# A hybrid SSD/S5 layer step in fp32 halves: z stored without SiLU, norm sums set between blocks of the first output product, S5 loads written one batch earlier

## The chip, the core and the metric

The kernel runs on one core of a Trainium2 chip. TensorE (PE) does the matrix products and takes its weights through a load step of its own (PEld); VectorE (DVE), ScalarE (ACT) and GpSimd (POOL) do the element-wise work; SyncE (SP) issues nearly all DMA transfers, in one queue, in the order of the program. The metric is the device time of one launch in microseconds. The time before is the median of three runs, 1028.26 us (1025.12 to 1031.12).

## What is computed

One step of one decoder layer for T = 1056 tokens: 1024 of a prompt, and 32 of 8 samples with 4 tokens each. Cut to what matters here:

```python
n = rmsnorm(h, g_in)
z_a, xbc, dt_raw, z_b, u_b = split(n @ w_in)
# A: Mamba-2 SSD, 16 heads in 2 groups of 512 channels
x, B, C = split(silu(causal_conv(xbc)))
y = ssd_scan(x, dt, A, B, C) + D * x
y = y * silu(z_a)
ya = y * rsqrt(mean(y * y, of its group) + eps) * ssd_norm_g
# B: S5, 64 groups of 16 channels, a complex diagonal state of 64 each
g = gelu(s5_scan(u_b))
yb = g * sigmoid(g @ glu_w + glu_b) * silu(z_b)
h = h + concat(ya, yb) @ w_out
h = h + (p @ w_ple_proj) * sigmoid(rmsnorm(h, g_ple) @ w_ple_gate)
return rmsnorm(h, g_final), states
```

`z_a` and `z_b` are needed only late, as the factors `silu(z)`; each is 1024 channels by 1056 tokens.

## The kernel before

Channels lie on the 128 partitions, tokens along the row. A dense product runs in fp32 split into a high and a low half, so each block is 24 matmuls: 8 slices of the contraction times three (high by high, high by low, low by high). Weights come by DMA in 128x512 pieces (`wr`), ACT rounds them to the high half (`wh`) and DVE subtracts to get the low half (`wl`). Activations go through the same split: `opn` is the pair of halves of an operand of the output product, its high half copied on ACT and its low half subtracted on DVE.

The order of the instructions on each engine is fixed when the kernel is built: a scheduler places them by modelled times under the dependencies of the program and some pins (`issue_after`, and `behind`, which sets an instruction behind a given one on its engine). On the chip each engine then runs its own list in order, and a waiting instruction holds all that stand behind it. Times below are microseconds from the start of the profiled span.

- To about 213: norm of the input, the u tiles, the S5 coefficients.
- 213 to 475: the convolution tiles and 16 batches of S5 (`s5_batch`), four channel groups each. A batch loads `u8`, `mm` (512 KB of matrices, from `md` in DRAM), `om` and `h8` from a pool of two buffers each, so the loads of batch n can begin when the last products of batch n-2 (`yp`) have read theirs. It starts on PE with the products `vi` and `vr` from `mm`.
- 475 to 656: the SSD recurrence in 16 units, and among it the rest of the z tiles. All 16 z tiles are products of 352 columns or fewer, evacuated by `z_evac`: ACT takes tanh(z/2) from PSUM, DVE forms (tanh + 1) * z, which is 2 silu(z), and the tile `zt` goes to DRAM (`zb_d` for j below 8, `za_d` above).
- 656 to 742 (and its m = 0 from 622 on, among the SSD units): the GLU, m = 0 to 7. The evacuation loads the z_b tile back (`gzl`) and `g` (`gg`), and DVE multiplies up to `yb`. After each m, `za_apply(m)` loads the z_a tile (`zl`, three pieces of 352 columns, called c0 to c2), multiplies it into `x` of that m on DVE, squares the product on ACT and adds the square to `ysq` on POOL. The tiles `zt`, `gzl`, `gg` and `zl` share one ring of six buffers.
- `ya_norm(g)` is the norm of SSD group g: sums of `ysq` over partitions as 12 matmuls of one column (`nsp`), a root by twelve short DVE operations (`nv`, `ny`, `nt`), a broadcast by 12 matmuls (`nrb`), and 12 DVE multiplications into `x`. `ya_norm(0)` follows m = 3, `ya_norm(1)` the loop.
- 742 to 913: the output product as seven products of half size (a Strassen form), each of 8 blocks of 24 matmuls with 264 columns, written in `PROD`. The first, `b11`, multiplies x of group 0 and yb 0 to 3; later ones need x of group 1. A block goes to one of eight PSUM banks, three of them the ones of `psb`, which `nrb` uses too.
- 913 to the end: the gate, the last product and the final norm.

Of the kernel before, what the change touches and what calls it, by code (L numbers as in the profile page):

```python
# [24 lines left out]
CW = 352  # L25
# [15 lines left out]
def hymba_ssd_s5_kernel(  # L41
# [216 lines left out]
    def rstd_tok(chunks, n, eps=EPS, after=None, pause=None):  # L258

        sp = psa("nsp")  # L260
        tw = chunks[0][0].shape[1]
        gr = -(-tw // 128)
        gr += tw % gr > 0
        qt, w = tw // gr, gr * len(chunks)
        for c, sqs in enumerate(chunks):

            for i, q in enumerate(sqs):
                if pause and i == len(sqs) - 1:
                    pe_end[0] = after
                    pause()  # L270
                    after = pe_end[0]
                for j in range(gr):
                    with behind(after):
                        end = PE.matmul(out=sp[0:qt, gr * c + j:gr * c + j + 1], lhsT=q[:, qt * j:qt * j + qt],  # L274
                                        rhs=ones[:, 0:1], start=(i == 0 and j == 0),
                                        stop=(i == len(sqs) - 1 and j == gr - 1))
                    if after is not None:
                        after = pe_end[0] = end
        v, y, t = (nw_p.tile([128, 16], F32, tag=q, name=q, bufs=b)[0:qt, 0:w]
                   for q, b in (("nv", 2), ("ny", 3), ("nt", 2)))  # L280
        ts(v, sp[0:qt, 0:w], 1.0 / n, eps, ALU.mult, ALU.add)
# [453 lines left out]
    def z_evac(j):  # L735
        dst = zb_d[j] if j < 8 else za_d[j - 8]

        def evac(c, t0, n, ps):
            t = ev("zt", n)
            if j >= 8:  # L740
                act(t, ps, AF.Tanh, scale=0.5)
                v_mid[0] = stt(t, t, 1.0, ps, ALU.add, ALU.mult)
                dma(out=dst[:, t0:t0 + n], in_=t)
                return

            nn = min(n, NPT - t0)
# [16 lines left out]
    def za_apply(j):  # L763
        for c in range(3):
            t0 = CW * c
            t = ev("zl")
            dma(out=t, in_=za_d[j, :, t0:t0 + CW])
            y = xs[j][:, t0:t0 + CW]
            mul(y, t, y)
            if j % 4 == 0:  # L770
                if c == 0:
                    ysq["t"] = cvt("ysq")
                ysq[c] = ysq["t"][:, t0:t0 + CW]
                act(ysq[c], y, AF.Square)
            else:
                act(t, y, AF.Square)
                add(ysq[c], ysq[c], t, G)
# [3 lines left out]
    NJ = NB // 2  # L781

    def s5_batch(b):
# [4 lines left out]
        u8 = s5.tile([128, NB, 144], F32, tag="u8", name="u8")  # L788
        dma(out=u8, in_=ud[:, :, g0:g0 + NB].rearrange("s h g c -> (s h) g c"))
        mm = s5.tile([128, NB, 2, 128], F32, tag="mm", name="mm")  # L790
        dma(out=mm, in_=md[:, g0:g0 + NB])
        tm, wv = mm[:, :, 0], mm[:, :, 1]
        om = s5.tile([128, NJ, 2, 128], F32, tag="om", name="om")
        dma(out=om, in_=od[:, j0:j0 + NJ])
        h8 = s5.tile([128, 2, NJ, 9], F32, tag="h8", name="h8")
        dma(out=h8, in_=s5h9[:, :, j0:j0 + NJ])
# [195 lines left out]

    def ya_norm(g):

        rt = rstd_tok([[ysq[c]] for c in range(3)], 512, 4 * EPS)
        for c in range(3):
            rs = rstd_bcast(rt[:, 4 * c:4 * c + 4])
            for i in range(4):
                y = xs[4 * g + i][:, CW * c:CW * c + CW]
                stt(y, y, vc[:, V_NG + 4 * g + i:V_NG + 4 * g + i + 1], rs, ALU.mult, ALU.mult)  # L1000
# [65 lines left out]
    for i, nm in enumerate(MID):  # L1066
# [84 lines left out]
    for m in range(8):  # L1151
# [3 lines left out]
        def evac(c, t0, n, ps):  # L1155
            z = ev("gzl", n)
            dma(out=z, in_=zb_d[m, :, t0:t0 + n])
            t = ev("zt", n)
# [9 lines left out]
            for yv, a, b, s, s0 in ((y[:, 0:NPT], 0, nn, 8, t0 // 128),) + (((y[:, NPT:T], nn, n, 4, 0),) if nn < n else ()):  # L1168
                zv, tv = (r[:, a:b].rearrange("p (s c) -> p s c", c=128 if s == 8 else 8) for r in (z, t))
                stt(yv.rearrange("p (c s) -> p s c", s=s)[:, s0:s0 + zv.shape[1]], zv, 0.25, tv, ALU.mult, ALU.mult)  # L1170
# [14 lines left out]
    def banks():  # L1185
        return [f("psd")[:, 0:CQ] for f in (lambda n: psd_(), lambda n: psd_(), lambda n: psd_(), psa, psa, psb, psb, psb)]
# [23 lines left out]
    for j, (wb, blk) in enumerate(PROD):  # L1210
        bk = banks()
        nxt = []
        for i in range(4):
            hi, lo = take_w((wb, i))
            w_split = list(last_split)
            for c in range(2):
                ps = bk[2 * i + c]
# [31 lines left out]
        opn = nxt  # L1249
# [190 lines left out]
```

## Time and profile before

| | us |
|---|---|
| median of three runs | 1028.26 |
| lowest, highest | 1025.12, 1031.12 |
| the profiled execution | 1028.4 |
| its span, first to last instruction | 1026.6 |
| PE busy | 996.4 (97%) |
| DVE busy | 809.5 (79%) |
| ACT busy | 454.6 (44%) |
| POOL busy | 164.9 (16%) |
| granted clock of TensorE, mean | 0.994 |

The profiled execution agrees with the median to 0.1 us, so a sum made against it needs no scaling. PE's share says how little of the span is left to win: 30 us in which PE stood still. Busy time of the other engines matters only where PE waits for them. The granted clock is the share of full speed at which the chip let TensorE run; a stretch at 0.5 is one at the lower of its two levels.

### The profile page before, as it was taken

To read this page: it belongs to the slowest core of one execution; us is meant where nothing else is said; L and a number is where in the kernel's file an instruction comes from. 1 tells how busy PE (TensorE), PEld (TensorE's weight loads), DVE (VectorE), ACT (ScalarE), POOL (GpSimd) and SP (SyncE) were. 2 spreads that over 40 slices of the span, in tenths; PEclk is the share of its full clock that TensorE was granted. 3 is DMA by queue.
4 is the path that set the end of the run, shared out by engine and by line. 5 is a ranking of instruction groups with operands and counts; after the bars stand their busy time and mean duration, and the time that the engine had idled before them with its cause. 6 is when DMAs were issued, how large, how long until landed. Compare 5 with 4: busy or idle time off the path is not lost.

```text
span 1026.6 us, 19644 instructions
## 1 busy us (share of the span) xinstructions
PE 996.4 (97%) x7214; PEld 945.3 (92%) x7214; DVE 809.5 (79%) x1880; ACT 454.6 (44%) x1009; POOL 164.9 (16%) x183
## 2 busy tenths in 40 slices
PE   9999999999999989999999997999999999999997
PEld 8999999979899989899887886899999999999996
DVE  5889989675998978984687768868778879986466
ACT  5733223345453434354865436344345435464221
POOL 0000000000000000002144233121232015641221
PEclk9999999999999989999999999999999999999999
DMA  9633489774658687755366668675634323335123
GB/s 315 219 77 120 148 254 245 198 244 132 196 168 255 193 236 206 207 155 183 113 185 200 204 189 224 170 201 166 176 114 136 112 90 125 120 114 171 50 95 106
DMA packets 181072, 174.89 MB, mean 170 GB/s; under 512 B 47728, under 2 KB 145520, under 8 KB 180976
## 3 DMA queue, kind: packets, MB, share of 16 engines
q1 hardware_dynamic: 150944, 153.23, 50.1%
q10 hardware_dynamic: 30032, 20.40, 6.4%
q8 instruction: 57, 0.93, 0.4%
q14 instruction: 39, 0.32, 0.1%
HBM read 123.05 MB, written 54.73 MB: 173 GB/s over the span
## 4 chain that ended last, share of the span: by engine, by line
PE 54%; DVE 8%; DMA 6%; issue 4%; ACT 2%; SPq 1%; POOL 0%; POOLq 0%; DVEq 0%; ACTq 0%
PE psd L233 30%; PE psd L1221 15%; DMA mm<-md 2%; PE yp L312 2%; ACT ab L77 1%; DMA ab<-acs_d 1%; PE nrb L296 1%; PE yd L873 1%; DVE acc L92 1%; PE yo L922 1%; DMA gr<-gd 1%; PE st L925 1%; DVE x L92 1%; DVE sst L80 1%; PE nsp L274 1%
## 5 line engine op out<-in xcount | busy, mean ns | idle before, releaser
L233 PE MATMUL psd<-n_h,wl 128*128 128x352 f32 x840 | 274.3, 327 | 1.4 <-DVE wl L80 1.4
L233 PE MATMUL psd<-n_h,wh 128*128 128x352 f32 x840 | 274.8, 327 | 0.0
L233 PE MATMUL psd<-n_l,wh 128*128 128x352 f32 x840 | 274.5, 327 | 0.0
L1221 PE MATMUL psd<-opn,wh 128*128 128x264 f32 x896 | 164.6, 285 | 1.7 <-DVE opn L80 1.7
L233 PEld LDWEIGHTS psd<-n_h,wh 128*128 128x128 f32 x840 | 158.7, 189 | 6.4 <-issue 6.1
L233 PEld LDWEIGHTS psd<-n_h,wl 128*128 128x128 f32 x840 | 158.7, 189 | 5.6 <-issue 3.4
L233 PEld LDWEIGHTS psd<-n_l,wh 128*128 128x128 f32 x840 | 158.7, 189 | 3.2 <-issue 2.9
L1221 PEld LDWEIGHTS psd<-opn,wh 128*128 128x128 f32 x896 | 138.8, 188 | 2.1 <-DVE opn L80 2.1
L80 DVE TENSOR_TENSOR wl<-wr,wh 128x512 fp32r<-128x512 f32 x146 | 106.3, 755 | 39.4 <-ACT wh L77 34.1
L77 ACT ACTIVATE wh<-wr 128x512 fp32r<-128x512 f32 x147 | 85.4, 622 | 105.5 <-PE psd L233 64.9
L1221 PE MATMUL psd<-opn,wl 128*128 128x264 f32 x448 | 127.1, 284 | 0.0
L1221 PEld LDWEIGHTS psd<-opn,wl 128*128 128x128 f32 x448 | 84.3, 188 | 0.0
L77 ACT ACTIVATE ab<-ab,tok 128x128 f32<-128x128 f32 (+1 forms) x144 | 42.9, 379 | 51.7 <-DMA ab<-acs_d 37.0
L233 PE MATMUL psd<-g_h,wh 128*128 128x384 f32 (+1 forms) x168 | 54.4, 324 | 0.0
L233 PE MATMUL psd<-g_l,wh 128*128 128x384 f32 (+1 forms) x168 | 54.0, 321 | 0.0
L233 PE MATMUL psd<-g_h,wl 128*128 128x384 f32 (+1 forms) x168 | 53.9, 321 | 0.0
L233 PE MATMUL psd<-hg_h,gwh 128*128 128x400 f32 (+1 forms) x144 | 46.7, 324 | 0.0
L233 PE MATMUL psd<-hg_l,gwh 128*128 128x400 f32 (+1 forms) x144 | 46.4, 322 | 0.0
L233 PE MATMUL psd<-hg_h,gwl 128*128 128x400 f32 (+1 forms) x144 | 46.3, 322 | 0.0
L77 ACT ACT_TABLE_LOAD x27 | 34.6, 1283 | 25.0 <-DVE acc L92 12.6
L92 DVE SCALAR_TENSOR_TENSOR zt<-zt,psd 128x352 f32<-128x352 f32 (+2 forms) x56 | 25.9, 463 | 23.3 <-ACT zt L77 23.0
L80 POOL TENSOR_TENSOR xl<-xl,h 128x264 f32<-128x264 f32 x32 | 29.8, 936 | 84.1 <-DMA xl<-xT 34.9
(323 smaller groups left out, 2044.3 us busy)
## 6 DMA issues: line engine op xcount, KB each, us to landing
wr<-wall SPq DMA_DIRECT2D x128, 256.0 KB, 3.4
mm<-md SPq DMA_DIRECT2D x16, 512.0 KB, 5.9
wa<-wall SPq DMA_DIRECT2D x32, 256.0 KB, 4.5
ws_d<-wa SPq DMA_DIRECT2D x16, 512.0 KB, 5.1
ab<-acs_d SPq DMA_DIRECT2D x16, 512.0 KB, 5.0
wr<-ws_d SPq DMA_DIRECT2D x32, 256.0 KB, 2.8
ud<-ub ACTq DMA_DIRECT2D x8, 576.0 KB, 4.8
u<-ud SPq DMA_DIRECT2D x16, 288.0 KB, 5.0
```

The lines of the kernel that those rows point to most:

```text
L77: return S.activation(out=out, in_=in_, func=func, **kw)
L80: return (eng or V).tensor_tensor(out=out, in0=a, in1=b, op=op)
L92: return V.scalar_tensor_tensor(out=out, in0=a, scalar=s, in1=b, op0=op0, op1=op1)
L233: end = PE.matmul(out=ps, lhsT=a[:, ko + k, :], rhs=b, start=(i == 0), stop=(i == 3 * K - 1))
L274: end = PE.matmul(out=sp[0:qt, gr * c + j:gr * c + j + 1], lhsT=q[:, qt * j:qt * j + qt], rhs=ones[:, 0:1], start=(i == 0 and j == 0), sto ...
L296: end = PE.matmul(out=rb[:, qt * j:qt * j + qt], lhsT=y[:, j:j + 1].to_broadcast([qt, 128]), rhs=ident[0:qt, 0:qt], start=True, stop=True)
L312: self.last = f(*a, **kw)
L873: PE.matmul(out=yd[64 * (e % 2):64 * (e % 2) + 64, e // 2], lhsT=x1[:, e], rhs=mt[:, e], start=True, stop=True)
L922: PE.matmul(out=yo[:, i], lhsT=hg[:, 128 * i:128 * i + 128], rhs=ct[g][:, cols], start=True, stop=True)
L925: PE.matmul(out=st, lhsT=bk, rhs=x2.rearrange("p e q -> p (e q)"), start=True, stop=True)
L1221: PE.matmul(out=ps, lhsT=a[:, k, :], rhs=b, start=(k == 0 and q == 0), stop=(k == 7 and q == 2))
```

## The change

Three things are rewritten. First, `z_evac` stores z as it comes from the product (one ACT copy, no DVE step), and SiLU is taken on ACT after the tile has been loaded back: on `gzl` in the GLU, and on `zl` in `za_apply`. The factors that made up for 2 silu(z) go (0.25 to 0.5, and 4 eps to eps). The additions into `ysq` go from POOL to DVE. Second, `ya_norm(1)` is cut into pieces written among the blocks of the first output product and pinned there: the `nsp` sums of c0, c1 and c2 directly behind blocks 0, 1 and 2, the root after the third, all `nrb` broadcasts behind block 4. The operands and the order of the second product are turned so that its yb half comes first; `ya_norm(0)` moves from behind m = 3 to ahead of `za_apply(4)`. Third, the loads of an S5 batch are a function `s5_load`, called for the next batch at the end of the loop step before.

```diff
-    def rstd_tok(chunks, n, eps=EPS, after=None, pause=None):
+    def rstd_tok(chunks, n, after=None, pause=None):
...
+        return rstd_root(sp[0:qt, 0:w], n)
...
         def evac(c, t0, n, ps):
             t = ev("zt", n)
             if j >= 8:
-                act(t, ps, AF.Tanh, scale=0.5)
-                v_mid[0] = stt(t, t, 1.0, ps, ALU.add, ALU.mult)
+                act(t, ps)
                 dma(out=dst[:, t0:t0 + n], in_=t)
                 return
...
-                act(v, pv, AF.Tanh, scale=0.5)
-                v_mid[0] = stt(v, v, 1.0, pv, ALU.add, ALU.mult)
+                act(v, ps[:, a:b].rearrange("p (c s) -> p s c", s=ns))
...
             t = ev("zl")
             dma(out=t, in_=za_d[j, :, t0:t0 + CW])
+            act(t, t, AF.Silu)
             y = xs[j][:, t0:t0 + CW]
             mul(y, t, y)
...
-                add(ysq[c], ysq[c], t, G)
+                add(ysq[c], ysq[c], t)
...
+    def s5_load(b):
+        s5, g0, j0 = s5c_["p"], NB * b, NB * b // 2
...
+        s5c_[b] = u8, mm, om, h8
 
     def s5_batch(b):
...
+        if b not in s5c_:
+            s5_load(b)
+        u8, mm, om, h8 = s5c_.pop(b)
...
             s5_batch(nb)
             nb += 1
+        if i > 2 and nb < 16:
+            s5_load(nb)
...
             z = ev("gzl", n)
             dma(out=z, in_=zb_d[m, :, t0:t0 + n])
+            act(z, z, AF.Silu)
...
         yb.append(y)
+        if m == 4:
+            ya_norm(0)
         za_apply(m)
-        if m == 3:
-            ya_norm(0)
-        if m in (4, 5):
-            opn += operand("b11", range(4 * (m - 4), 4 * (m - 4) + 4))
-
-
-    ya_norm(1)
+        if m == 4:
+            opn = operand("b11", range(4, 8))
+        if m == 5:
+            opn = operand("b11", range(4)) + opn
...
+    def ya_piece(n):
+        if n < 3:
+            if n == 0:
+                ya1["sp"] = psa("nsp")
+            for j in range(4):
+                with behind(pe_end[0]):
+                    pe_end[0] = PE.matmul(out=ya1["sp"][0:88, 4 * n + j:4 * n + j + 1],
+                                          lhsT=ysq[n][:, 88 * j:88 * j + 88], rhs=ones[:, 0:1],
+                                          start=(j == 0), stop=(j == 3))
+        if n == 2:
+            ya1["rt"] = rstd_root(ya1["sp"][0:88, 0:12], 512)
+        if n == 4:
+            for c in range(3):
+                ya_scale(1, c, ya1["rt"])
...
-                        PE.matmul(out=ps, lhsT=a[:, k, :], rhs=b, start=(k == 0 and q == 0),
-                                  stop=(k == 7 and q == 2))
+                        with behind(pe_end[0] if j == 0 and 0 < 2 * i + c < 6 else None):
+                            end = PE.matmul(out=ps, lhsT=a[:, k, :], rhs=b, start=(k == 0 and q == 0),
+                                            stop=(k == 7 and q == 2))
+                        if j == 0 and 2 * i + c < 6:
+                            pe_end[0] = end
+                if j == 0 and 2 * i + c < 5:
+                    ya_piece(2 * i + c)
...
-                    nxt += operand(PROD[j + 1][1], range(2 * i, 2 * i + 2))
+                    nxt += operand(PROD[j + 1][1], [(2 * i + q + (4 if j == 0 else 0)) % 8 for q in range(2)])
...
-        opn = nxt
+        opn = nxt[4:] + nxt[:4] if j == 0 else nxt
```

What it moves, by the built order of the two kernels. PE, in the first output product, before (the third block, whose start waits for its weights, and then the norm sums of all three pieces, which wait for POOL):

```order
L1221 MATMUL psd<-opn,wh 128x264 [waits Activation_49]
L1221 MATMUL psd<-opn,wh 128x264
L1221 MATMUL psd<-opn,wl 128x264 [waits DVE_49]
...
L1221 MATMUL psd<-opn,wl 128x264 [waits DVE_49]
L274 MATMUL nsp<-cs,ysq 88x1 [waits Pool_49]
L274 MATMUL nsp<-cs,ysq 88x1 x3
```

PE at the end of the first block of that product, after:

```order
L1255 MATMUL psd<-opn,wh 128x264 x2
L1255 MATMUL psd<-opn,wl 128x264
L1213 MATMUL nsp<-cs,ysq 88x1 [waits DVE_49]
L1213 MATMUL nsp<-cs,ysq 88x1 x3
L1255 MATMUL psd<-opn,wh 128x264 [waits Activation_49]
L1255 MATMUL psd<-opn,wh 128x264
L1255 MATMUL psd<-opn,wl 128x264
```

The first sums have moved from the middle of the third block to the end of the first, ahead of the whole second block, and wait for DVE in place of POOL. ACT at the end of the GLU, before (`zt` is the GLU's last evacuation, `h4` the first product block's, `zl` from `x7` the three squares of `za_apply(7)`):

```order
L77 ACTIVATE wh_8774<-wr_8771 128x512 [waits DMAHW4_49]
L77 ACTIVATE zt_8675<-psd_8648,glb_5612 128x288 [waits DMAHW5_49,DMAHW2_49,DMAHW6_49,DVE_49,PE_49]
L77 ACTIVATE h4_8757<-psd_8762 128x264 [waits PE_49]
L77 ACTIVATE zl_8683<-x7_5345 128x352 [waits DMAHW3_49,DVE_49,Activation_49]
L77 ACTIVATE zl_8688<-x7_5345 128x352 [waits DMAHW4_49,DMAHW7_49,DVE_49,Pool_49]
L77 ACTIVATE zl_8693<-x7_5345 128x352 [waits DMAHW5_49,DVE_49]
```

and after:

```order
L77 ACTIVATE zt_8664<-psd_8636,glb_5580 128x288 [waits DMAHW5_49,PE_49]
L77 ACTIVATE zl_8672<-zl_8672 128x352 [waits DMAHW3_49,DVE_49]
L77 ACTIVATE h4_8694<-psd_8709 128x264 [waits PE_49]
L77 ACTIVATE opn_8770<-yb4_8091 128x528
L77 ACTIVATE opn_8773<-yb5_8289 128x528
L77 ACTIVATE zl_8678<-zl_8678 128x352 [waits DMAHW7_49,DMAHW4_49,DVE_49]
L77 ACTIVATE zl_8684<-zl_8684 128x352 [waits DMAHW5_49]
L77 ACTIVATE zl_8672<-x7_5325 128x352 [waits DVE_49]
```

The square of c0 now stands behind three Silus, the copy out of block 0 and two operand copies; on DVE the addition of c0 into `ysq` stands behind the two operand subtractions and the multiplications of c1 and c2 in the same way. SP in the convolution stage, around the loads of one S5 batch (n = 9), before:

```order
L181 DMA wa<-wall 128x2x256 [waits DMAHW6_49]
L162 DMA wr<-wall 128x512 [waits DMAHW7_49,DVE_49]
L794 DMA om<-od 128x512 [waits PE_49]
L789 DMA u_4378<-ud 128x576 [waits PE_49]
L791 DMA mm<-md 128x1024 [waits DMAHW2_49]
L852 DMA gd<-yt 128x544 [waits DMAHW3_49,Activation_49]
```

and after:

```order
L162 DMA wr<-wall 128x512 [waits DMAHW6_49,DVE_49]
L162 DMA wr<-wall 128x512 [waits DMAHW7_49,DVE_49]
L792 DMA om<-od 128x512 [waits DMAHW0_49,PE_49]
L788 DMA u_4241<-ud 128x576 [waits DMAHW1_49,PE_49]
L790 DMA mm<-md 128x1024 [waits DMAHW2_49]
L861 DMA gd<-yt 128x544 [waits DMAHW3_49,Activation_49]
```

The loads stand at the same place in the queue, between the weight loads and the store of `gd`, and still behind a wait for PE, which is the release of the buffers by batch n-2.

## Rows read from the trace of the kernel before

**Rows 1.** The page, busy time of each engine, share, instructions.

```profile
PE 996.4 (97%) x7214; PEld 945.3 (92%) x7214; DVE 809.5 (79%) x1880; ACT 454.6 (44%) x1009; POOL 164.9 (16%) x183
```

**Rows 2.** Busy time by stage: stretch, length, each engine's busy us (instructions), clock, DMA.

```profile
620.00:656.00 36.00, 29.24 (x195) 23.39 (x196) 33.63 (x60) 16.46 (x39) 13.05 (x9) 0.95 0.76 204
656.00:742.00 86.00, 86.00 (x557) 85.52 (x556) 64.67 (x130) 33.34 (x66) 16.07 (x16) 1.00 0.67 189
742.00:770.00 28.00, 28.00 (x242) 28.00 (x241) 21.88 (x47) 13.05 (x27) 7.95 (x9) 1.00 0.37 112
```

**Rows 3.** Waits of PE, whole span: waiter, releaser, us in total, times, longest.

```profile
PE vi L309 <- DMA mm<-md: 6.5, 4, 2.9
PE psd L247 <- ACT g_h L77: 3.9, 4, 2.4
...
PE psd L233 <- DVE wl L80: 1.4, 1, 1.4
PE vi L309 <- DVE tb L80: 1.2, 1, 1.2
```

**Rows 4.** The tile mm, its 16 loads.

```profile
DMA to landing us min/median/max: 4.8/5.9/6.8
```

**Rows 5.** Timeline, S5 batch 9: start, us, engine, line, operation [idle before].

```profile
354.83 0.38 PE L312 MATMUL yp<-u,mm 128*128 128x136 f32 x1
...
359.11 0.43 SPq L791 DMA_DIRECT2D mm<-md  x1
...
365.60 0.46 PE L309 MATMUL vi<-u,mm 128*64 128x136 f32 x1 [2.90 <-DMA mm<-md]
```

**Rows 6.** Timeline, end of the GLU and first output product.

```profile
742.18 0.40 PE L1221 MATMUL psd<-opn,wh 128*128 128x264 f32 x2
...
742.82 1.40 SPq L767 DMA_DIRECT2D zl<-za_d  x3
...
743.30 0.48 ACT L77 ACTIVATE zt<-psd,glb 128x288 f32<-128x288 f32 x1
...
745.29 0.39 ACT L77 ACTIVATE h<-psd 128x264 f32<-128x264 f32 x1 [1.51 <-PE psd L1221]
...
745.57 1.07 DVE L80 TENSOR_TENSOR x<-zl,x 128x352 f32<-128x352 f32 x2
...
747.40 0.74 DVE L80 TENSOR_TENSOR x<-zl,x 128x352 f32<-128x352 f32 x1 [0.77 <-DMA zl<-za_d]
...
749.87 1.97 PE L274 MATMUL nsp<-cs,ysq 128*88 128x1 f32 x24
...
758.34 5.99 DVE L92 SCALAR_TENSOR_TENSOR x<-x,vc,nrb 128x352 f32<-128x352 f32 x12 [0.43 <-PE nrb L296]
```

**Rows 7.** Groups by line and shape: count, busy us, mean ns, idle before.

```profile
L77 ACT ACTIVATE opn<-yb 128x528 fp32r<-128x528 f32 x28 | 17.2, 643 | 16.5 <-DVE yb L80 16.5
L80 DVE TENSOR_TENSOR opn<-yb,opn 128x528 fp32r<-128x528 f32 x28 | 20.8, 789 | 0.0
L80 DVE TENSOR_TENSOR x<-zl,x 128x352 f32<-128x352 f32 x24 | 12.6, 551 | 3.9 <-DMA zl<-za_d 3.5
L77 ACT ACTIVATE zl<-x 128x352 f32<-128x352 f32 x18 | 8.8, 496 | 22.2 <-DVE x L80 21.3 <-DMA wr<-wall 0.8
L77 ACT ACTIVATE zt<-psd 128x352 f32<-128x352 f32 x40 | 18.1, 451 | 19.5 <-PE psd L233 18.0 <-issue 1.4
L92 DVE SCALAR_TENSOR_TENSOR zt<-zt,psd 128x352 f32<-128x352 f32 (+2 forms) x56 | 25.9, 463 | 23.3 <-ACT zt L77 23.0
L77 ACT ACT_TABLE_LOAD x27 | 34.6, 1283 | 25.0 <-DVE acc L92 12.6
```

**Rows 8.** Busy time of two stretches behind a wait, columns as in rows 2.

```profile
365.00:371.00 6.00, 5.40 (x27) 5.07 (x28) 2.00 (x6) 1.22 (x4) 0.00 (x0) 0.50 1.03 228
371.00:374.00 3.00, 3.00 (x18) 3.00 (x18) 3.00 (x12) 0.78 (x4) 0.00 (x0) 0.87 0.36 96
638.00:642.00 4.00, 4.00 (x22) 3.72 (x19) 3.97 (x11) 3.53 (x12) 1.19 (x1) 0.57 0.70 182
```

More of the change, by code (lines that the diff above doesn't have):

```diff
@@ L278, in rstd_tok, with rstd_root @@
                         after = pe_end[0] = end
+        return rstd_root(sp[0:qt, 0:w], n)
+    def rstd_root(sp, n):
+        qt, w = sp.shape
         v, y, t = (nw_p.tile([128, 16], F32, tag=q, name=q, bufs=b)[0:qt, 0:w]
                    for q, b in (("nv", 2), ("ny", 3), ("nt", 2)))
-        ts(v, sp[0:qt, 0:w], 1.0 / n, eps, ALU.mult, ALU.add)
+        ts(v, sp, 1.0 / n, EPS, ALU.mult, ALU.add)
         ts(y.bitcast(I32), v.bitcast(I32), 1, None, ALU.logical_shift_right)
@@ L748, in evac @@
                 v = t[:, a:b].rearrange("p (s c) -> p s c", s=ns)
-                pv = ps[:, a:b].rearrange("p (c s) -> p s c", s=ns)
-                act(v, pv, AF.Tanh, scale=0.5)
-                v_mid[0] = stt(v, v, 1.0, pv, ALU.add, ALU.mult)
+                act(v, ps[:, a:b].rearrange("p (c s) -> p s c", s=ns))
                 o = dst[:, 0:NPT] if d0 == 0 else dst[:, NPT:T]
@@ L776, in za_apply @@
                 act(t, y, AF.Square)
-                add(ysq[c], ysq[c], t, G)
+                add(ysq[c], ysq[c], t)
     NB = 4
     NJ = NB // 2
+    def s5_load(b):
+        s5, g0, j0 = s5c_["p"], NB * b, NB * b // 2
+        u8 = s5.tile([128, NB, 144], F32, tag="u8", name="u8")
+        dma(out=u8, in_=ud[:, :, g0:g0 + NB].rearrange("s h g c -> (s h) g c"))
+        mm = s5.tile([128, NB, 2, 128], F32, tag="mm", name="mm")
+        dma(out=mm, in_=md[:, g0:g0 + NB])
+        om = s5.tile([128, NJ, 2, 128], F32, tag="om", name="om")
+        dma(out=om, in_=od[:, j0:j0 + NJ])
+        h8 = s5.tile([128, 2, NJ, 9], F32, tag="h8", name="h8")
+        dma(out=h8, in_=s5h9[:, :, j0:j0 + NJ])
+        s5c_[b] = u8, mm, om, h8
     def s5_batch(b):
@@ L787, in s5_batch @@
         j0 = g0 // 2
[L788 to L791, printed above, removed]
+        if b not in s5c_:
+            s5_load(b)
+        u8, mm, om, h8 = s5c_.pop(b)
         tm, wv = mm[:, :, 0], mm[:, :, 1]
[L793 to L796, printed above, removed]
         vr, vi = psa("vr"), psa("vi")
@@ L990, in sample_end, with ya_scale @@
             ssd_y(8, g, 32, yds[g], yo)
+    def ya_scale(g, c, rt):
+        rs = rstd_bcast(rt[:, 4 * c:4 * c + 4], pe_end[0])
+        for i in range(4):
+            y = xs[4 * g + i][:, CW * c:CW * c + CW]
+            stt(y, y, vc[:, V_NG + 4 * g + i:V_NG + 4 * g + i + 1], rs, ALU.mult, ALU.mult)
     def ya_norm(g):
-        rt = rstd_tok([[ysq[c]] for c in range(3)], 512, 4 * EPS)
+        pe_end[0] = None
+        rt = rstd_tok([[ysq[c]] for c in range(3)], 512)
         for c in range(3):
[L997 to L1000, printed above, removed]
+            ya_scale(g, c, rt)
     s5_es, sd_es = ExitStack(), ExitStack()
@@ L1169, in evac @@
                 zv, tv = (r[:, a:b].rearrange("p (s c) -> p s c", c=128 if s == 8 else 8) for r in (z, t))
-                stt(yv.rearrange("p (c s) -> p s c", s=s)[:, s0:s0 + zv.shape[1]], zv, 0.25, tv, ALU.mult, ALU.mult)
+                stt(yv.rearrange("p (c s) -> p s c", s=s)[:, s0:s0 + zv.shape[1]], zv, 0.5, tv, ALU.mult, ALU.mult)
         (dense_k if m == 0 else dense)(w, g_h, g_l, evac, chunks=PCH)
         yb.append(y)
+        if m == 4:
+            ya_norm(0)
         za_apply(m)
-        if m == 3:
-            ya_norm(0)
-        if m in (4, 5):
-            opn += operand("b11", range(4 * (m - 4), 4 * (m - 4) + 4))
-    ya_norm(1)
+        if m == 4:
+            opn = operand("b11", range(4, 8))
+        if m == 5:
+            opn = operand("b11", range(4)) + opn
     h_r = [row(f"h{m}") for m in range(8)]
@@ L1183, in hymba_ssd_s5_kernel, with bank @@
     hg_h, hg_l = [None] * 8, [None] * 8
-    def banks():
-        return [f("psd")[:, 0:CQ] for f in (lambda n: psd_(), lambda n: psd_(), lambda n: psd_(), psa, psa, psb, psb, psb)]
+    def bank(n):
+        return (psd_() if n < 3 else psa("psd") if n < 5 else psb("psd"))[:, 0:CQ]
+    ya1 = {}
+    def ya_piece(n):
[12 more added lines that the diff above has]
+                ya_scale(1, c, ya1["rt"])
     def hg_split(m):
@@ L1210, in hymba_ssd_s5_kernel @@
     for j, (wb, blk) in enumerate(PROD):
-        bk = banks()
         nxt = []
@@ L1216, in hymba_ssd_s5_kernel @@
             for c in range(2):
-                ps = bk[2 * i + c]
+                ps = bank(2 * i + c)
                 for k in range(8):
```

## The prediction

> **What bounds the kernel now.** I read the busy shares first: PE is busy 996.4 of 1026.6 us [rows 1], so about 30 us are all that any rearrangement can win, and every stop that is added to PE costs its full length. Then the stages: in the GLU (656 to 742) and in the first output product (742 to 770) PE has no idle time at all, while DVE works 64.67 of 86 and 21.88 of 28 us and ACT less than half [rows 2]. Only the end of the SSD (620 to 656) is set by DVE, 33.63 of 36 us. Then PE's waits: the largest group is 6.5 us for the S5 matrices `mm`, and two waits for DVE of 1.4 and 1.2 us are about what z's DVE work could have to do with [rows 3]. Last, what stood behind the two longest waits: after 2.90 us for `mm` at 365.60 [rows 5] TensorE runs at 0.50 from 365 to 371 and 0.87 to 374, and after a wait of 2.4 us [rows 3] it runs at 0.57 from 638 to 642 [rows 8]. So a stop of PE has a second price.
>
> **z without SiLU.** Removed: 56 DVE operations, 25.9 us [rows 7]. The ACT operation beside each stays (a copy for a tanh, 451 ns for 352 columns). DVE is not the limit where most of them run, and the waits that could shrink are the 1.4 and the 1.2 us of rows 3; I count 0, with -1.5 as the bound. Added: 48 Silus on ACT, 24 on `gzl` and 24 on `zl`, by the copy's 451 ns about 21 us. ACT has 52 us free in the GLU, where it is busy 33.34 of 86 [rows 2], so its load is covered; what is not covered is the latency, one operation more between the landing of a tile and its use, in a ring of six buffers that twelve tiles go through in each m. Each of the two is 0.45 us on a chain of a few us in a period of about 11.5 us (86 us for seven and a half m), so I count 0 here, too; without that cover, half a microsecond for each m, up to 4.
>
> The 18 additions into `ysq` go from POOL to DVE, at some 551 ns each like the multiplication of the same shape [rows 7] 10 us, less than half of what the 56 gave back; they are hidden in the GLU. The order of the new kernel has five table loads more on ACT, of 1283 ns [rows 7], 6.4 us in all, two of them around the exponentials of the SSD's end, where ACT is busy 16.46 of 36 us [rows 2]. I count 0 and keep 2.6 as the bound for two that fall on the path.
>
> On the table loads the Trainium skill, "ScalarE: Activation LUTs", section "What ACT_TABLE_LOAD costs", says that a switch costs the 1283 ns load and about 1380 ns of drain, some 2.66 us together. The trace agrees on the load [rows 7] and shows no drain as a row of its own. By the page the five are 13.3 us of ACT (an estimate from its figures) and the two at the SSD's end up to 5.3 us, with which the sum below would be at most 5.3 us longer; it speaks against moving SiLU to where tanh is used, if ACT were late.
>
> **S5 loads.** They are written a batch earlier, but the pool still has two buffers. By the order the three loads stand where they stood on SP, behind the release by batch n-2 and the weight loads. The trace shows that this is what they wait for: the last `yp` of batch 7 starts at 354.83, the load of batch 9 is issued at 359.11, PE wants it by 362.7 and gets it at 365.60 [rows 5], and the transfer alone takes 4.8 to 6.8 us [rows 4]. Seven batches had a short stretch of PE work between the two before, and seven have one after, not the same ones. So the 7.7 us of waits (6.5 and 1.2 [rows 3]) are dealt anew and not removed: 0, from -7.7 (and the clock's 3.1 at 365, below) to +4 for the batch whose `mm` now stands behind four weight loads.
>
> **Norm sums in the first output product.** Here the change adds a wait. Before, all twelve sums stood in the third block at 749.87 and PE did not wait for them [rows 6]. Now those of c0 stand directly behind block 0, and seven blocks and all later products are queued behind them. Block 0 starts at 742.18 and its result is read at 745.29 [rows 6], so PE arrives at about 745.1. When is `ysq` of c0 ready? On before's clock ACT goes, in the new order: Silu of c0 when it has landed, near 745.5 (its multiplication begins at 745.57 [rows 6]), to 746.0; the copy of block 0, 0.39, to 746.4; two operand copies of 0.643 [rows 7], to 747.7; Silus of c1 and c2, 0.45 each, to 748.6 (c2 has landed at 747.40 [rows 6]); the square of c0, 0.50 [rows 7], to 749.1. DVE goes: the second operand subtraction, 0.789, from 747.7 to 748.5; the multiplications of c1 and c2, 0.55 each, to 749.6; the addition, 0.5, to 750.1. PE stands from 745.1 to 750.1: **+5.0 us**. The lower bound is ACT's queue from 745.3 without a wait for data: 0.39 + 1.29 + 0.90 + 0.50 and the addition, 748.9, a stop of 3.7. The upper one has the loads of `zl`, issued at 742.82 [rows 6], 1.5 us later because three more Silus sit in the ring ahead of them: 6.5. The sums of c1 and c2 follow in 0.5 us steps and are ready when their blocks end.
>
> **The clock after it.** The two stops of 2.9 and 2.4 us that rows 8 show were each followed by a slow stretch; one of 5 us would be, too. Its price: 0.50 x 5.40 + 0.13 x 3.00 = 3.1 us at 365 and 0.43 x 4.00 = 1.7 us at 638. I take the middle, **+2.4**, with 0 to 3.1 as bounds.
>
> **The broadcasts.** The twelve `nrb` stand between blocks 4 and 5 in place of inside block 4, the same work. Block 5's bank is one that `nrb` of c0 used, and so it waits for c0's four multiplications. Before, the first of twelve began 1.1 us after the broadcasts and the twelve took 5.99 [rows 6], 0.5 each: c0 is done 3.1 us after they begin. The broadcasts occupy PE 2.5 us: **+0.5** (0 to 1). `ya_norm(0)`, moved by one m, has its sums and broadcasts amid GLU products as before: 0.
>
> **Sum.** Against the profiled execution, which the median matches: 1028.4 + 5.0 + 2.4 + 0.5 = 1036.3, given as 1036.
>
> **Rivals.** *Not slower: the S5 waits go.* If the loads are in time, 7.7 us of waits and the 3.1 us of slow clock at 365 are gone: 1036.3 - 10.8 = 1025.5. It decides where the load is issued: if 7 us ahead of `vi` in every batch, the gain is whole. Against it stands the buffer wait in SP's order; for it, that the new order is another one and may happen to give each batch room. This would be the change doing what it says.
> *The sums find their data ready.* If `zl` comes early enough that c0 is added up by 745.1, the stop and the slow clock fall away: 1028.9. That needs three Silus, two operand copies and the square to run ahead of block 0's end, and the copy of block 0 in ACT's row, which cannot run ahead of it, speaks against it.
> *The clock holds.* The stop alone: 1033.9. For it: the two slow stretches differ by almost a factor of two, so what stands around the wait counts as well, and PE is at work without a break before this one; against it, both of the longest waits have such a stretch behind them.
> *Silus late.* The upper stop of 6.5 and 4 us more from the S5 deal or from the ring: 1036.3 + 1.5 + 4 = 1041.8.
> *Both good cases*, neither stop nor S5 waits: 1028.4 - 10.8 = 1017.6.
>
> **How the numbers follow.** Chances: the forecast 0.50, S5 waits gone 0.12, sums ready 0.10, clock holds 0.11, Silus late 0.12, both good 0.05. About 0.5% of 1028.26, 5.1 us, is what a measurement of this kernel can tell from no change, so faster means under 1023.1 and slower over 1033.4. Faster: 0.05 and a little of the S5 case, 0.07. Slower: 0.48 of the forecast, 0.06 of the held clock, 0.12: 0.66. The same: the rest, 0.27. The range reaches from 1025.5, which leaves out the both-good case and half of the S5 one, to 1042, which leaves out half of the late Silus: 0.17 outside.
>
> **What would show it.** Right: a wait of PE at the first product's first `nsp`, 4 to 6 us, released by DVE; a stretch at about half clock behind it; `vi` waiting for `mm` for 5 to 10 us over the span, in other batches; the GLU still without PE idle; DVE's busy time down by about 15 us and ACT's up by about 25. Wrong: no wait at `nsp`; no waits for `mm`; PE idle in the GLU; or `mm` issued ahead of the release by batch n-2.

## The result and the profile after

The changed kernel takes 1040.68 us, the median of four runs (1038.26 to 1043.38), against 1029.69 for the kernel before in the same comparison (1025.12 to 1033.97). The ratio is 1.0114 with a 95% interval from 1.0079 to 1.015: slower by 11.7 us by the ratio (11.0 by the two medians), where the forecast said 7.7 slower and 1036. The profiled execution took 1038.26 us with a span of 1036.5, 9.9 us more than the one of before.

The page of the changed kernel, busy time of each engine (beside [rows 1]):

```profile
PE 1000.4 (97%) x7214; PEld 949.2 (92%) x7214; DVE 791.9 (76%) x1842; ACT 480.8 (46%) x1062; POOL 146.6 (14%) x165
```

DVE has lost 17.6 us and ACT gained 26.2, as the forecast had it. PE's waits over the whole span (beside [rows 3]) show where the time went: what led the list before, `vi` waiting for the load of `mm`, is down to one wait of 2.0 us, put down to DVE, and a single wait of 9.4 us has come in.

```profile
PE nsp L1213 <- DVE ysq L80: 9.4, 1, 9.4
...
PE psd L682 <- DVE wh L80: 2.1, 1, 2.1
PE nsp L274 <- DVE ysq L80: 2.0, 1, 2.0
PE vi L313 <- DVE wa L80: 2.0, 1, 2.0
```

Busy time by stage (stretch, length, PE, PEld, DVE, ACT, POOL in us, clock, DMA; beside [rows 2]): the GLU, which had no idle PE, has two microseconds of it, and of the 28 us from 742 PE works 18.61, at a mean clock of 0.76.

```profile
656.00:742.00 86.00, 83.97 (x543) 83.64 (x541) 61.03 (x127) 47.43 (x102) 0.00 (x0) 0.98 0.60 169
742.00:770.00 28.00, 18.61 (x139) 18.62 (x139) 15.36 (x37) 10.50 (x24) 4.99 (x5) 0.76 0.43 123
```

The timeline of the place (beside [rows 6]): start, length, operation, and in brackets the idle time ahead of it (SPq is the queue of SP).

```profile
738.89 0.41 PE L1255 MATMUL psd<-opn,wh 128*128 128x264 f32 x2
...
743.70 2.10 SPq L768 DMA_DIRECT2D zl<-za_d  x3
...
745.04 0.44 ACT L77 ACTIVATE gzl<-gzl 128x288 f32<-128x288 f32 x1 [2.93 <-DVE yb L92]
...
746.43 0.48 ACT L77 ACTIVATE zt<-psd,glb 128x288 f32<-128x288 f32 x1
746.81 0.48 ACT L77 ACTIVATE zl<-zl 128x352 f32<-128x352 f32 x1
747.20 0.37 ACT L77 ACTIVATE h<-psd 128x264 f32<-128x264 f32 x1
747.47 1.17 ACT L77 ACTIVATE opn<-yb 128x528 fp32r<-128x528 f32 x2
748.53 0.87 ACT L77 ACTIVATE zl<-zl 128x352 f32<-128x352 f32 x2
749.30 0.49 ACT L77 ACTIVATE zl<-x 128x352 f32<-128x352 f32 x1
...
751.38 1.33 PE L1213 MATMUL nsp<-cs,ysq 128*88 128x1 f32 x8 [9.42 <-DVE ysq L80]
...
771.28 0.64 PE L1255 MATMUL psd<-opn,wh 128*128 128x264 f32 x2 [0.45 <-DVE x L92]
```

The product starts at 738.89, 3.3 us earlier than before. From there to the end of the span it takes 297.6 us in place of 284.4, 13.2 more. So one subtraction splits the 9.9 us: 3.3 gained up to the first product, 13.2 lost behind it. Of the 13.2, 9.4 are the wait and 0.45 the wait of block 5 behind the broadcasts. The slow clock behind the stop is worth 0.50 x 5.62 + 0.13 x 3.00 = 3.2, and a second slow stretch, behind the broadcasts, 0.43 x 3.72 = 1.6, by these rows of the stretches (columns as above):

```profile
751.00:757.00 6.00, 5.62 (x28) 5.62 (x29) 1.20 (x3) 0.43 (x1) 1.28 (x1) 0.50 0.29 83
757.00:760.00 3.00, 3.00 (x26) 3.00 (x26) 1.29 (x2) 1.43 (x3) 0.50 (x1) 0.87 0.00 0
771.00:775.00 4.00, 3.72 (x18) 3.75 (x19) 4.00 (x10) 1.18 (x2) 0.00 (x0) 0.57 0.02 4
```

Against that, PE's waits for operands near the end of the output product are 1.2 us shorter; first the kernel before, then the changed one:

```profile
PE psd L1221 <- DVE opn L80: 1.7, 2, 1.2
PE psd L1255 <- DVE opn L80: 0.5, 1, 0.5
```

Together these are 13.5 us, which accounts for the 13.2.

### The profile page after: what moved, and what is told of

It is laid out like the page before. It is cut to its first block, busy times and chain, and to the rows that moved or that the text cites. A ratio compares the mean times of both kernels' runs of the same rounds, so it can differ in the third digit from the quotient of the medians.

```text
span 1036.5 us, 19618 instructions
## 1 busy us (share of the span) xinstructions
PE 1000.4 (97%) x7214; PEld 949.2 (92%) x7214; DVE 791.9 (76%) x1842; ACT 480.8 (46%) x1062; POOL 146.6 (14%) x165
## 4 chain that ended last, share of the span: by engine, by line
PE 73%; DVE 11%; DMA 9%; issue 3%; ACT 3%; SPq 0%; POOL 0%; POOLq 0%; DVEq 0%; ACTq 0%
PE psd L233 44%; PE psd L1255 15%; PE yp L316 2%; DMA gg<-gd 2%; DVE x L92 2%; DVE yb L92 1%; DMA zl<-za_d 1%; PE yd L882 1%; PE st L934 1%; DMA gzl<-zb_d 1%; ACT ab L77 1%; PE yo L931 1%; DVE wl L80 1%; PE kp L316 1%; DMA wr<-wall 1%
## 5 line engine op out<-in xcount | busy, mean ns | idle before, releaser
L1255 PE MATMUL psd<-opn,wh 128*128 128x264 f32 x896 | 167.9, 289 | 1.0 <-DVE opn L80 0.5
L80 DVE TENSOR_TENSOR wl<-wr,wh 128x512 fp32r<-128x512 f32 x146 | 100.8, 721 | 56.9 <-ACT wh L77 55.8
L1255 PEld LDWEIGHTS psd<-opn,wh 128*128 128x128 f32 x896 | 141.8, 192 | 1.3 <-DVE opn L80 0.8
L80 POOL TENSOR_TENSOR xl<-xl,h 128x264 f32<-128x264 f32 x32 | 32.9, 1031 | 196.6 <-DMA xl<-xT 140.5
L77 ACT ACT_TABLE_LOAD x32 | 41.1, 1283 | 23.7 <-DVE acc L92 11.7
```

Of the source, the lines that this page charges most:

```text
L77: return S.activation(out=out, in_=in_, func=func, **kw)
L80: return (eng or V).tensor_tensor(out=out, in0=a, in1=b, op=op)
L1255: end = PE.matmul(out=ps, lhsT=a[:, k, :], rhs=b, start=(k == 0 and q == 0), stop=(k == 7 and q == 2))
```

## The experiments

Below, the stop is PE's wait at the first sums of the second group, and an engine's row is its list of instructions in order. Theory: two parts of the change make the 9.4 us together. The pins put the sums where PE arrives before the data, worth some 5 us by the forecast's reckoning, and SiLU at the use makes the data later than that reckoning had it. What is gained ahead of the product comes from z's part, not from the S5 loads. Rivals: the pins alone make 9.4; the ring of six buffers is what is late; the S5 loads make the gain. Ratios are to the kernel before, run on the same chip. A wait in a trace belongs to one execution.

### The norm in one piece again

```diff
+    ya_norm(1)
     h_r = [row(f"h{m}") for m in range(8)]
...
-                        with behind(pe_end[0] if j == 0 and 0 < 2 * i + c < 6 else None):
+                        with behind(None):
...
-                if j == 0 and 2 * i + c < 5:
-                    ya_piece(2 * i + c)
```

> The changed kernel with the norm of the second SSD group written in one piece ahead of the products again, so that the scheduler places its sums and broadcasts where it likes; z without SiLU, the S5 loads and the place of the first group's norm stay changed. Theory (the pinned place makes the 9.4 us stop, and the slow clock behind it costs 3 us more): the stop shrinks to what is left when the sums of c0 stand behind block 2, about 3 us, and the time is about 1029 to 1031. Rival (the data is late wherever the sums stand, since the GLU's evacuation lags): the stop stays above 6 us and the time above 1036.

Measured: 1.0076 (1.0052 to 1.01), 1031.43 us. The scheduler put the sums of c0 behind the third block and the others into the fourth. The largest single wait at them is 1.4 us, and about 2 us more are waits for the GLU's last evacuations. So the pins make most of the stop. Of the time they make less: from 1.0114 to 1.0076 it is some 4 of the 11.7 us, and the two intervals overlap. The time is a little over what was expected, and something else of the change still costs.

### The norm part alone, and z alone, and the S5 loads alone

Each is the kernel before with one of the three parts of the diff.

> The kernel before with the norm part of the change alone: the pinned pieces behind blocks 0, 1, 2 and 4, the turned operands, the first group's norm moved to m = 4; z is stored with SiLU and the additions stay on POOL, the S5 loads are as before. Theory (of the 9.4 us some 5 come from the pinned place and the rest from the SiLU that now sits in the chain of every tile): a stop of 3.5 to 5 us at the first sums, 2 us of slow clock, about 1035. Rival (the place alone): a stop of 9 us and about 1042.

Measured: 1.0095 (1.0064 to 1.0125). The stop is 4.7 us, and it is released by POOL:

```profile
PE nsp L1212 <- POOL ysq L80: 4.7, 1, 4.7
```

The theory holds: without SiLU at the use, the pins make a stop of about the size that the forecast had reckoned (5.0). The agreement is not of like with like, since the forecast's chain counted three Silus and an addition on DVE, and here the additions are still on POOL.

> The kernel before with z stored without SiLU alone (SiLU on ACT at the use, the additions into ysq on DVE); norm and S5 loads as before. Theory (the extra operation makes the evacuation of the GLU late by some 4 us at its end, DVE's relief buys nothing): a stop of 0 to 3 us at the first sums although they stand in the third block, mm waits as before, 1029 to 1033. Rival (DVE's relief lets the S5 chains and the loads behind them run earlier and takes the waits for mm away): waits for mm under 3 us and about 1022.

Measured: 1.0034 (1.0004 to 1.0064). Neither side is quite right. The waits for `mm` fall to 1.8 us, as the rival said, but the time does not fall with them: PE waits 3.9 us at the sums of the first group's norm in the GLU, and the clock behind falls to half (these stretches are 692 to 705):

```profile
PE nsp L274 <- DVE ysq L80: 3.9, 3, 1.9
```

```profile
692.00:696.00 4.00, 2.18 (x17) 1.86 (x15) 3.43 (x9) 3.20 (x7) 0.00 (x0) 1.00 0.65 198
696.00:699.00 3.00, 0.88 (x9) 0.80 (x9) 1.35 (x3) 0.83 (x2) 0.00 (x0) 0.81 0.59 179
699.00:702.00 3.00, 3.00 (x16) 3.00 (x17) 2.51 (x10) 0.61 (x2) 0.00 (x0) 0.50 0.71 155
702.00:705.00 3.00, 3.00 (x15) 3.00 (x15) 0.76 (x5) 0.00 (x0) 0.00 (x0) 0.55 0.35 123
```

z's part wins in the convolution stage and loses more in the GLU.

> The kernel before with the S5 loads alone written one batch earlier. By the prediction (the two buffers keep the loads behind batch n-2, so the waits are dealt anew): 5 to 10 us of waits for mm, 1029 plus or minus 3. Rival (the changed kernel's drop of these waits from 7.7 to 2.0 us is the work of this part): waits for mm of about 2 us and about 1022.

Measured: 1.0006 (0.9971 to 1.0042). No difference that can be told; `vi` waits 5.8 us (3.3 for `mm`, the rest put down to DVE) and 2.4 more ahead of the first batch. The forecast's reading of the loads holds: written earlier, they are not issued earlier.

### The changed kernel with the S5 loads at their old place

```diff
-        if i > 2 and nb < 16:
-            s5_load(nb)
```

> The changed kernel with the S5 loads written at their old place, inside the batch that uses them; z without SiLU and the pinned pieces stay. Theory (the loads' place in the program does nothing, since the two buffers hold them, and the drop of the waits in the S5 stage is DVE's relief): the waits of vi stay at 2 to 3 us in all, the stop stays at 9 us, the time at 1040 plus or minus 3. Rival (the earlier loads have their part in the drop): the waits of vi rise to 6 us or more and the time to 1044 or more.

Measured: 1.0096 (1.0052 to 1.0139). `vi` waits 1.7 us and the stop is 9.1 us, as in the changed kernel. The loads' part does nothing there either. As to the time, 1.0096 and 1.0114 have intervals that lie over each other; in microseconds, 1035.4 (kernel before: 1026.4), it lies under the 1040 plus or minus 3 that was expected.

### z stored as its tanh, the DVE operation left out

```diff
                 act(t, ps, AF.Tanh, scale=0.5)
-                v_mid[0] = stt(t, t, 1.0, ps, ALU.add, ALU.mult)
...
                 act(v, pv, AF.Tanh, scale=0.5)
-                v_mid[0] = stt(v, v, 1.0, pv, ALU.add, ALU.mult)
```

> The kernel before without the 56 DVE operations that make silu out of tanh (z is stored as its tanh alone, so the output lacks this factor); nothing is added anywhere. Theory (z's part took the mm waits down from 7.7 to 2 us by relieving DVE in the convolution stage, and lost more than that in the GLU by SiLU at the use): mm waits under 3 us, no stop in the GLU, 3 to 6 us faster than before, some of the gain given back at the start of the SSD, where PE then waits for DVE. Rival (the waits for mm are only dealt anew by any other order): waits of 5 us or more and no gain.

Measured: 0.9946 (0.9921 to 0.9971), faster by 5.5 us. One wait of 1.8 us is left at `vi`, and in the GLU PE has no idle time. So taking the 56 operations away is a gain, together with the order that the scheduler then makes.

### The changed kernel without its SiLUs

```diff
             t = ev("zl")
             dma(out=t, in_=za_d[j, :, t0:t0 + CW])
-            act(t, t, AF.Silu)
...
             dma(out=z, in_=zb_d[m, :, t0:t0 + n])
-            act(z, z, AF.Silu)
```

> The changed kernel with both SiLU operations left out (z multiplies in raw, so the output lacks this factor); pinned pieces, S5 loads and all else as in the changed kernel. Theory (a SiLU at the use puts the waits for the loads of gzl and zl into ACT's queue, ahead of the work behind it, and that makes the GLU's evacuation late): ACT no longer waits for these loads, ysq of c0 is ready 8 us after the first product starts in place of 12.4, the stop falls from 9.4 to 4 to 5 us, the stop of the first group's norm in the GLU goes, and the time is about 1029. Rival (the lag comes from the pins and the additions on DVE): the stop stays near 9 and the time above 1036.

Measured: 1.0044 (1.0011 to 1.0076), 1032.8 us, so the expected 1029 was missed. The expected signs in the trace came: the stop is 5.1 us in place of 9.4, the first group's norm no longer stops PE, and `ysq` of c0 is ready 8.1 us behind the product's start in place of 12.4.

```profile
PE nsp L1211 <- DVE ysq L80: 5.1, 1, 5.1
```

The tanh of the GLU's last chunk (`zt`) and the loads of `zl` start 1.1 and 1.6 us behind the product (741.09); in the changed kernel they start 7.5 and 4.8 us behind it.

```profile
742.22 0.49 ACT L77 ACTIVATE zt<-psd,glb 128x288 f32<-128x288 f32 x1
...
742.70 2.14 SPq L768 DMA_DIRECT2D zl<-za_d  x3
```

So 4.3 of the 9.4 us come from the SiLUs at the use. The way there is read from what ACT waits for from 656 to 750. In the changed kernel:

```profile
ACT gzl L77 <- DMA gzl<-zb_d: 13.6, 10, 3.7
ACT zl L77 <- DMA zl<-za_d: 13.1, 9, 3.0
ACT zt L77 <- DVE yb L92: 5.0, 3, 4.7
ACT gzl L77 <- DVE yb L92: 4.5, 2, 2.9
```

and without the SiLUs:

```profile
ACT zl L77 <- DVE x L80: 24.0, 9, 5.2
ACT zt L77 <- PE psd L233: 7.7, 3, 6.2
ACT wh L77 <- PE psd L233: 7.1, 5, 2.4
```

There it is DVE that waits for the loads:

```profile
DVE x L80 <- DMA zl<-za_d: 4.4, 6, 1.4
DVE gzl L92 <- DMA gzl<-zb_d: 2.1, 2, 1.3
```

An operation at the use is not only 0.5 us longer a chain. It is the first one that touches the loaded tile, so the wait for the load moves from DVE to ACT, and ACT's row holds what the next tile needs: the tanh of the next chunk, the copy of a block, the split of the weights. 26.7 us of such waits are in the changed kernel and none in this one. ACT does not wait less in all without the SiLUs, as the 24.0 us of its squares show; what differs is what stands behind a wait. The 2.93 us ahead of the last `gzl` in the timeline are put down to DVE, but the trace has the load of this tile landing at 744.96, 0.08 us ahead of its Silu. This part of the account is argued from the traces: the run takes away the 48 operations (ACT is busy 33.24 us in the GLU in place of 47.43) together with the waits, and does not part the two. The ring has its share, too: from 728 to 752 of the changed kernel SP holds back loads of `gzl` and `gg` for 10.1 us, until an addition into `ysq` frees a buffer; without the SiLUs it is 6.8.

```profile
SPq L1180 <- DVE ysq L80: 6.0, 2, 3.5
SPq L1171 <- DVE ysq L80: 4.1, 3, 2.6
```

### Sums two blocks later

```diff
-        if n < 3:
-            if n == 0:
+        if 2 <= n < 5:
+            if n == 2:
...
-        if n == 4:
+        if n == 5:
             for c in range(3):
                 ya_scale(1, c, ya1["rt"])
```

> The changed kernel with its pinned pieces moved: sums behind blocks 2, 3 and 4 in place of 0, 1 and 2, the broadcasts behind block 5 in place of 4. Theory (the stop is the distance between PE's arrival and ysq of c0, and two blocks of 2.93 us are laid into it): the stop falls from 9.4 to 3.5 us and the time by 6 to 8, to about 1033. Rival (what delays ysq is the work queued on ACT and DVE for these blocks, which then comes earlier too): the stop stays above 6 us, 1037 or more.

Measured: 1.0061 (1.0035 to 1.0087). The stop is 1.3 us, and three short ones have come beside it: 1.2 us behind the broadcasts (block 6's bank now), 0.4 and 0.3. The theory holds for the stop, which even fell by more than the 5.9 us of two blocks: in this execution the loads of `zl` are issued 2.9 us behind the product's start (742.36 and 739.45) in place of 4.8. What is left, about 6 us over the kernel before by the ratio, is no longer in one place.

### The tanh in place in PSUM

```diff
-            t = ev("zt", n)
-            act(t, ps, AF.Tanh, scale=0.5, bias=glb[:, m:m + 1])
-            stt(z, t, 1.0, z, ALU.add, ALU.mult)
+            act(ps, ps, AF.Tanh, scale=0.5, bias=glb[:, m:m + 1])
+            stt(z, ps, 1.0, z, ALU.add, ALU.mult)
```

> The changed kernel with the GLU's tanh written in place in PSUM, so that no zt tile is taken: nine tiles in each m go through the ring of six buffers in place of twelve; pinned sums and all else as in the changed kernel. Theory (the evacuation of the GLU lags behind PE because the loads of gzl, gg and zl wait for a buffer of the ring, which the SiLU holds longer): the loads of zl for m = 7 are issued 3 us or more earlier against the first product's start, the stop falls from 9.4 to 5 us or less, about 1034. Rival (the lag is the latency of loads and of the engines' queues, not a lack of buffers): the stop stays at 8 to 10 us and the time at 1040.

Measured: 1.0085 (1.0054 to 1.0117), 1034.3 us. All the signs that the theory had named came: the stop falls to 1.3 us, the time is near 1034, and the loads of `zl` for m = 7 are issued 0.6 us ahead of the product's start in place of 4.8 behind it. They do not show the theory all the same. The loads are issued at 744.61, later than the 743.70 of the changed kernel; it is the product that starts later, at 745.21 in place of 738.89. In the GLU's products PE now waits for PSUM banks that DVE has still to read, and for the root of the first group's norm:

```profile
PE nrb L300 <- DVE ny L92: 2.7, 1, 2.7
PE psd L233 <- DVE gzl L92: 2.5, 2, 2.1
```

The stop was moved, and the ring of buffers is not shown to be the limit. No run gave the ring more buffers, so its part stays open. The time cannot be told from that of the changed kernel: the two intervals overlap.

> The last two together: sums behind blocks 2 to 4 and the tanh in place in PSUM. If both theories hold nothing of the stop is left and z's gain in the convolution stage stays: about 1025. If only the place matters: 1033.

Measured: 1.0114 (1.0082 to 1.0147). With both, nothing is left of the stop at the sums, and the product starts at 749.59. All that had been saved was spent ahead of it; neither of the two expected times came.

### SiLU straight from PSUM

```diff
-                act(v, pv, AF.Tanh, scale=0.5)
-                v_mid[0] = stt(v, v, 1.0, pv, ALU.add, ALU.mult)
+                act(v, pv, AF.Silu)
...
-                stt(..., zv, 0.25, tv, ALU.mult, ALU.mult)
+                stt(..., zv, 0.5, tv, ALU.mult, ALU.mult)
```

> The kernel before with SiLU of the eight z_b tiles taken by ACT straight from PSUM at the evacuation (no DVE step, no SiLU at the use), the z_a tiles, norm and S5 loads as before. The built order has five table loads more on ACT, as the changed kernel. Theory (what pays is DVE's relief in the convolution stage, and it need not cost latency in the GLU): waits for mm under 4 us, no stop in the GLU, 3 to 5 us faster than before. Rival (the table switches hold up the S5 outputs and the conv tiles on ACT in this stage): new waits for ACT there, no gain or 2 us slower.

Measured: 0.9954 (0.9927 to 0.9982), a median of 1022.83 us over twelve runs against 1027.62. Nothing of the layer is left out here, and the run is faster than both kernels. `vi` waits 2.4 us, and the GLU and the product are as before:

```profile
656.00:742.00 86.00, 86.00 (x565) 86.00 (x564) 65.64 (x128) 33.24 (x65) 15.96 (x15) 1.00 0.66 185
742.00:770.00 28.00, 28.00 (x242) 28.00 (x241) 22.29 (x46) 11.89 (x25) 8.50 (x9) 1.00 0.41 123
```

> As the last one with the z_a tiles too, which fall among the exponentials of the SSD: 33 table loads more than before, 42 us of ACT at 1.28 us each. If ACT has the room (it is busy 81 of 145 us in that stage before): 5 us faster than before. If the switches lie on the path of the SSD's decay matrices: new waits of PE for DVE and ACT between 475 and 656, 5 us slower or more.

Measured: 1.0182 (1.0137 to 1.0227). By the trace 27 table loads stand between 475 and 660, among the exponentials of the SSD, where there was one. From 475 to 620 PE works 130.70 us where it worked 143.74 before, and its largest wait is put down to `cbm`, a tile of the SSD that DVE forms from the PSUM tile `cb`:

```profile
PE xt L909 <- DVE cbm L80: 8.0, 4, 2.8
```

DVE in turn waits for `bk`, a copy that ACT makes out of the same tile: 15.5 us from 475 to 656, against 3.1 before.

```profile
DVE cbm L80 <- ACT bk L77: 15.5, 5, 6.3
```

The stage, in the columns from above:

```profile
475.00:620.00 145.00, 130.70 (x873) 109.32 (x873) 76.32 (x130) 98.03 (x207) 41.25 (x36) 0.96 0.49 149
```

So ACT is late here, busy 98.03 us in place of 80.88. How much of the loss is the loads and how much the new order of ACT's row, this run does not part.

### The runs side by side

Start of the first product, time from it to the end of the span, wait at the first sums: of one profiled execution each. The ratio is of all runs of a kernel.

| kernel | product starts | from there to the end | stop | ratio |
|---|---|---|---|---|
| before | 742.18 | 284.4 | 0 | 1 |
| after | 738.89 | 297.6 | 9.4 | 1.0114 |
| norm in one piece | 740.08 | 289.6 | 1.4 | 1.0076 |
| norm alone | 738.34 | 292.2 | 4.7 | 1.0095 |
| z alone | 742.16 | 285.4 | 0.1 | 1.0034 |
| S5 loads alone | 740.00 | 284.5 | 0 | 1.0006 |
| S5 loads back | 736.72 | 296.3 | 9.1 | 1.0096 |
| SiLUs left out | 741.09 | 292.7 | 5.1 | 1.0044 |
| sums later | 739.45 | 289.2 | 1.3 | 1.0061 |
| tanh in PSUM | 745.21 | 286.4 | 1.3 | 1.0085 |
| both of these | 749.59 | 288.3 | 0 | 1.0114 |
| DVE step left out | 739.83 | 283.4 | 0.2 | 0.9946 |
| SiLU from PSUM, z_b | 739.74 | 283.8 | 0 | 0.9954 |
| SiLU from PSUM, all | 756.39 | 284.1 | 0 | 1.0182 |

The column behind the product agrees with the stop in the four kernels with a stop of 4.7 us or more: 284.4, plus the stop, plus 2.8 to 3.8 us for the clock, block 5 and the rest. The first column differs by 2.2 us between two kernels whose medians cannot be told apart (before and the S5 loads alone), so single values of it are not to be read more closely than that.

## Why the prediction was right, and where it was not

The way, the place and the order of size were right: a wait of PE at the first sums, released by DVE, a slow clock behind it, and a time within the range. That the time came out there is in part luck, as its steps show:

- **The stop, 5.0 us: mis-sized, 9.4.** The chain was right. From the landing of c0 to the sums it reckoned 4.6 us (745.5 to 750.1); by the trace c0 lands at 746.61 and the sums start at 751.38, which is 4.8. What failed is the start of the chain: it took the loads of `zl` as issued 0.64 us behind the product's start, as in [rows 6], with 1.5 us more at worst; they were issued 4.8 us behind it, and so the upper bound of 6.5 did not hold. (The lower one, 3.7, is 3.8 by its own terms.) In the time of the span the loads are only 0.9 us later than before (743.70 and 742.82); the rest is PE, which reached the product 3.3 us earlier while the loads did not. The forecast saw one operation more in a chain; what came was ACT's row waiting for loads, with 4.3 us of the stop. The pins without the SiLUs measured 4.7 and 5.1, and that this is so near to 5.0, which had Silus in it, is chance in part.
- **SiLU at the use, 0: wrong by some 4 us at the stop and 3.6 in the GLU.** The prediction said that only latency was not covered, and named half a microsecond for each m as the price without cover. The stop of 2.0 us at the first group's norm and its half-clock stretch (0.50 x 3.00 and a little, 1.6) are also this: they go when the SiLUs go. By the ratios the SiLUs cost some 7 us (1.0114 and 1.0044). `ya_norm(0)` had been counted at nothing.
- **z's DVE work, 0 with -1.5 as the bound: wrong.** It was worth 5.5 us (0.9946), be it by the relief or by the order that comes with it. The waits it could shrink were read off the list as the two with a DVE operation as releaser. But the S5 waits are down in every kernel without the step on z_b: 1.7 to 2.7 us at `vi` in eleven kernels, 5.8 to 7.7 in the three that have it.
- **S5 loads, 0: right.** 1.0006 alone, and no gain in the changed kernel. The fall of the waits that the first rival had priced came, but with another part of the change and not because the loads were written earlier. That rival had also said that the new order may happen to give each batch room; whether it is that stays open. With this fall, the forecast's total was closer than its terms.
- **The clock, 2.4 with 3.1 as the upper bound: mis-sized, 4.8.** 3.2 of it stood behind the stop, a little over the bound, and 1.6 behind the broadcasts, where the forecast had none. **The broadcasts, 0.5: 0.45**, within the bounds.
- **Table loads, 0: no loss was seen.** The kernel has 32 of them, 41.1 us, against 27 [rows 7]. In the z_b run five loads more stand between 213 and 475, and the time falls. No run has the two at the SSD's end alone; PE's waits for ACT's `g_h` there are 3.1 us, against the 3.9 of [rows 3].

The errors were of opposite sign: about 8 us more for the SiLUs and 2.4 for the clock, 5 to 6 less for z's step. That is why a sum of 1036 stood beside a median of 1041. With the error on the SiLUs alone it would have been 1044 (an estimate, 1036.3 and 8), outside the range.

What stays open: why the S5 waits fall. DVE is relieved in that stage, and at the same time the scheduler, with the step gone, lays the products in another order and no longer pins the weight sums behind z's last DVE operation. In batch 9, which waited 2.9 us before [rows 5], the changed kernel issues `mm` 3.1 us behind the start of the last `yp` (before 4.3), its products start at 347.09 in place of 365.60, and `vi` does not wait for that load. The one wait of 2.0 us that is left is put down to DVE and ends at 364.12; the load of `mm` for that batch (n = 10) landed 0.2 us earlier, so it may be a wait like those before. No run parts the relief from the order. Open, too, is what remains of about 6 us when the sums come two blocks later, and what the turned operands and the moved first norm cost by themselves: they are in the run with the norm in one piece (1.0076) and not in z alone (1.0034), and these intervals overlap.

## What to carry to other kernels

A step that is moved from the producer to the consumer takes the wait for the load with it: ask which engine is now the first to touch the loaded tile, and what stands behind that in its row. Work that is pinned to a place on the bottleneck engine is paid for in full when its data is late, so a pin needs the latest time of its data, not the time of an undisturbed trace. And to price a term of nothing, look for the run that has this part alone: here two terms of nothing hid 8 us of loss and 5 us of gain.

## What was not expected of the hardware

A switch of ACT's tables cost little more than its load. The Trainium skill, "ScalarE: Activation LUTs", section "What ACT_TABLE_LOAD costs", puts a drain of about 1380 ns beside the 1283 ns load. In the run with 60 loads the operation before a load ends 0.02 us ahead of it and the next begins 0.01 us behind it, as medians; here is one of them (start, length; 534.23 + 1.28 is 535.51):

```profile
533.53 0.68 ACT L77 ACTIVATE bb<-bh,cs 96x128 fp32r<-96x128 f32 x2
534.23 1.28 ACT L77 ACT_TABLE_LOAD   x1
535.52 0.47 ACT L77 ACTIVATE zt<-psd 128x352 f32<-128x352 f32 x1
```

So the trace shows 1.3 us for a switch and not 2.66; here the measurement decides. The clock fell in a place where PE had not stopped, too. With z's part alone, behind sums that had waited 0.1 us, the granted clock of 751 to 757 was 0.75 and 0.68 with PE busy throughout. (The kernel before has the same sums at 749.87 [rows 6] and kept 1.00 there [rows 2].) The rows:

```profile
751.00:754.00 3.00, 3.00 (x27) 3.00 (x27) 2.90 (x7) 0.87 (x3) 2.47 (x2) 0.75 0.73 211
754.00:757.00 3.00, 3.00 (x19) 3.00 (x19) 1.39 (x9) 0.00 (x0) 0.00 (x0) 0.68 0.39 117
```

And it fell during a stop, before PE resumed: the granted clock of 748 to 751 in the changed kernel, within the 9.4 us, was 0.50 with no matmul at all.

```profile
748.00:751.00 3.00, 0.00 (x0) 0.00 (x0) 3.00 (x8) 2.30 (x7) 0.00 (x0) 0.50 0.92 279
```
